# Eighteen of 22 pairs of ffn-up chunks as seven half-size products in place of eight

## The chip, the cores and the metric

The kernel runs on one core of a Trainium2 chip. The metric is the time of one execution on the device in microseconds (us); lower is better. Matrix products run on TensorE (PE in the profile; its weight loads are PEld), elementwise work on VectorE (DVE), ScalarE (ACT) and GpSimd (POOL). SP, the sync engine, issues most of the DMA transfers. Each engine takes its instructions in a fixed order and waits on semaphores for the others.

## The reference

The program is one step of a two-layer transformer for 128 context tokens and 512 latent tokens (640 columns in all, 1024 features). Each layer is an attention sub-layer and then a gated feed-forward layer ("ffn") with a width-3 convolution over the tokens:

```
def conv_ffn(u, w_up, conv_w, conv_b, w_down):
    z = u @ w_up                                   # 1024 -> 2 * 2816
    zp = jnp.pad(z, ((0, 0), (1, 1), (0, 0)))
    z = zp[:, :-2] * conv_w[0] + zp[:, 1:-1] * conv_w[1] + zp[:, 2:] * conv_w[2] + conv_b
    gate, val = jnp.split(z, 2, axis=-1)
    return (jax.nn.silu(gate) * val) @ w_down      # 2816 -> 1024
```

Its input u is the normalised residual stream h, scaled and shifted by vectors that depend on the conditioning ("adaLN"); its output is normalised, gated and added to h. The change touches z = u @ w_up alone.

## The kernel before

Activations lie with the features on the 128 partitions and the 640 tokens along the free axis, in eight chunks k of 128 features. All numbers are float32; a product keeps that precision by splitting each operand into a high part (a copy rounded to float32r, made by ACT) and a low part (operand minus high part, a subtraction of two SBUF operands on DVE or POOL): `split`, lines 160 to 162. Each product is then three matmuls, high by high, high by low, low by high.

The 2816 hidden features are 22 chunks of 128, each with a gate and a value chunk: a pair. `ffn_up` computes one pair. For each of its two chunks `chunks` loads 128x1024 weights, splits them (`load_w`), and `proj` runs 8 k times 3 matmuls times 2 halves of 320 tokens, 48 matmuls a chunk and 96 a pair, into one PSUM tile (`pu`). The input of these products is not yet normalised (class `Raw`), so `take` multiplies the result by the norm's reciprocal on DVE while it leaves PSUM, and ACT adds the shift. `conv` is one ACT instruction (line 1348) and six scalar_tensor_tensor on DVE (line 1356), which read `za` twice. After the second chunk: silu (ACT), gate times value (DVE, line 1387), and a split of the product g.

`ffn_down` follows part by part: the 22 pairs are cut into PARTS, the down product of a part (8 output chunks `dn`, n pairs times 6 matmuls each) stands behind the first pair of the next part, and its result is added to `yf` on DVE. The last part goes through `product` (`dl`) together with the closing norm and residual. `Pace` spreads the adaLN products (`ada`, weights `wm`) over the pairs.

A scheduler that has its own estimate of every instruction sets the order on each engine and the places in memory; the code's order is a priority to it. PSUM and SBUF tiles come from rings of a fixed count (`bufs`): raw weights `wr` 2 or 3, split weights `wh` and `wl` 3 each, adaLN weights `wm` 4.

Of the kernel before, what the change touches and what calls it, by code (L numbers as in the profile page):

```python
# [10 lines left out]
F32 = mybir.dt.float32  # L11
# [8 lines left out]
NCTX = 128  # L20
# [9 lines left out]
PARTS = [5, 6, 6, 5]  # L30
# [26 lines left out]
def tile_step(ctx: ExitStack, tc: tile.TileContext, a: dict):  # L57
# [9 lines left out]
    def dr(name, dt=F32):  # L67
        return dw(name, dt)[:, 0:1280]
# [77 lines left out]
    def load_w(src, n, name, kept=False, low=None):  # L146
        raw = wt("wr", f"wr_{name}")
        SP.dma_start(raw[:, :n], src)
        if kept:
            if n == 640:  # L150
                hl = dr(f"wk_{name}", F32R)
                hi, lo = hl[:, 0:n], hl[:, n : 2 * n]
            else:
                hi, lo = (dr(f"wk{v}_{name}", F32R) for v in range(2))
        else:
            hi, lo = wt("wh", f"wh_{name}", F32R), wt("wl", f"wl_{name}", F32R)
        split(raw[:, :n], hi[:, :n], lo[:, :n], low or DVE)
        return hi, lo
# [396 lines left out]
    def score_steps(pr):  # L555
# [17 lines left out]
        def dense(m, g):  # L573
# [6 lines left out]
            pd = wt(("wh", "wl")[g], f"p{pr.name}{m}{g}") if g < 2 else pr.kt4[:, m * 512 : m * 512 + 512]  # L580
# [791 lines left out]
    def ffn_up(l, u, c, first, pace):  # L1372
# [16 lines left out]
        split(t[0], g[:, 0:640], g[:, 640:1280])  # L1389
        return (g[:, 0:640], g[:, 640:1280])  # L1390
# [105 lines left out]
    for l in range(2):  # L1496
# [235 lines left out]
```

## Time and profile before

| | |
|---|---|
| runs | 1892.93, 1895.81, 1897.44 us, median 1895.81 us |
| the profiled execution | 1893.93 us, of which the span (first to last instruction) is 1891.8 us |
| busy: PE, PEld, DVE, ACT, POOL | 96%, 83%, 54%, 43%, 13% of the span |
| the ffn of layer 0 | about 504 to 945 us of the span |
| the ffn of layer 1 | about 1412 to 1838 us |

Busy time is the union of an engine's records. Matmuls are pipelined, so the mean duration of one (311 ns for 320 columns) is about twice the step from one to the next; the pace is read from a stretch, time by count. On DVE too an instruction's record begins a little before the one ahead of it ends when neither waits. PEclk is the TensorE clock that was granted, as a share of 2.4 GHz.

### The profile page before, as it was taken

The numbers are of one execution on the slowest core, as the hardware profiler recorded it, in microseconds if no ns is written. First come the engines' busy times: TensorE is split into PE (matmuls) and PEld (weight loads), VectorE is DVE, ScalarE is ACT, GpSimd is POOL, SyncE is SP. The second block draws the span as 40 slices with busy tenths as digits, with TensorE's granted clock in tenths as the row PEclk, the third lists the DMA queues.
The fourth block names the chain that finished last, engine by engine and source line by source line (L and its number), as shares of the span: only waits on it lengthen the run. The fifth ranks groups of instructions, "written<-read, shape, count | busy, mean of one in ns | idle before, by whom it ended". The sixth has DMA issues, their size and how long they took to land.

```text
span 1891.8 us, 28912 instructions
## 1 busy us (share of the span) xinstructions
PE 1818.3 (96%) x11619; PEld 1577.3 (83%) x11619; DVE 1025.9 (54%) x1776; ACT 806.2 (43%) x1325; POOL 253.9 (13%) x247
## 2 busy tenths in 40 slices
PE   7989799999999999999989998999999999999997
PEld 4888555569799999999978985456979999999996
DVE  3453454564663563663665644435467456466365
ACT  3433233255553451542465533324555345244245
POOL 0011243343100000000030003630220000000002
PEclk8999899999999999999999998999989999999999
DMA  7656564233133333333233364573412222222213
GB/s 254 195 159 219 146 184 119 77 128 140 68 96 96 114 104 121 124 120 101 95 104 126 116 212 147 167 205 113 152 67 86 94 79 65 82 78 62 84 58 105
DMA packets 84101, 229.88 MB, mean 122 GB/s; under 512 B 12224, under 2 KB 24896, under 8 KB 83968
## 3 DMA queue, kind: packets, MB, share of 16 engines
q1 hardware_dynamic: 74656, 209.73, 34.7%
q10 hardware_dynamic: 6720, 7.82, 1.5%
q0 software_dynamic: 2592, 10.49, 1.5%
q8 instruction: 91, 1.49, 0.3%
q14 instruction: 42, 0.34, 0.1%
HBM read 198.82 MB, written 28.06 MB: 120 GB/s over the span
## 4 chain that ended last, share of the span: by engine, by line
PE 81%; DVE 4%; issue 2%; DMA 2%; ACT 2%; POOL 1%; ACTq 0%; SPq 0%; POOLq 0%; DVEq 0%
PE pu L187 32%; PE dn L187 13%; PE op L187 2%; PE ada L321 2%; PE poD L638 2%; PE pnq L187 2%; PE pnk L187 1%; PE poG L638 1%; PE stM L569 1%; PE stG L569 1%; PE pqc L187 1%; PE poM L638 1%; PE stD L569 1%; PE dl L187 1%; PE op L166 1%
## 5 line engine op out<-in xcount | busy, mean ns | idle before, releaser
L187 PE MATMUL pu<-uop,wh_u 128*128 128x322 f32 (+1 forms) x2688 | 512.6, 312 | 0.0
L187 PEld LDWEIGHTS pu<-uop,wh_u 128*128 128x128 f32 x2688 | 428.7, 190 | 5.8 <-ACT wh_u L161 4.1
L187 PE MATMUL pu<-uop,wl_u 128*128 128x322 f32 x1344 | 308.2, 311 | 0.0
L1356 DVE SCALAR_TENSOR_TENSOR za<-za,cst 128x127 f32<-128x127 f32 (+1 forms) x528 | 193.1, 435 | 91.2 <-ACT za L1348 91.1
L187 PEld LDWEIGHTS pu<-uop,wl_u 128*128 128x128 f32 x1344 | 224.8, 188 | 0.0
L187 PE MATMUL dn<-g,wh_d 128*128 128x320 f32 x1088 | 203.8, 309 | 0.3 <-DVE cst L330 0.3
L291 POOL TENSOR_TENSOR cst<-cst 128x352 f32<-128x352 f32 (+4 forms) x42 | 48.1, 1145 | 1044.3 <-ACT cst L1427 1041.8
L187 PEld LDWEIGHTS dn<-g,wh_d 128*128 128x128 f32 x1088 | 170.8, 188 | 0.8 <-ACT wh_d L161 0.4
L161 ACT ACTIVATE wh_u<-wr_u 128x1024 fp32r<-128x1024 f32 x88 | 93.4, 1062 | 145.8 <-PE pu L187 73.0
L187 PE MATMUL dn<-g,wl_d 128*128 128x320 f32 x544 | 124.1, 309 | 0.0
L162 DVE TENSOR_TENSOR wl_u<-wr_u,wh_u 128x1024 fp32r<-128x1024 f32 x84 | 102.4, 1220 | 20.7 <-ACT wh_u L161 20.5
L437 ACT ACTIVATE za<-za,cst 128x128 f32<-128x128 f32 (+1 forms) x176 | 89.4, 556 | 22.8 <-DVE za L435 22.0
L187 PEld LDWEIGHTS dn<-g,wl_d 128*128 128x128 f32 x544 | 90.9, 188 | 0.0
L161 ACT ACTIVATE wh_d<-wr_d 128x768 fp32r<-128x768 f32 (+1 forms) x48 | 38.9, 811 | 113.1 <-PE dn L187 98.6
L1348 ACT ACTIVATE za<-za,cst 128x640 f32<-128x640 f32 x88 | 81.2, 923 | 3.0
L161 ACT ACTIVATE g<-za 128x640 fp32r<-128x640 f32 x44 | 32.5, 738 | 115.0 <-DVE za L1387 115.0
L434 DVE COPY cst<-pu 128x2 f32<-128x2 f32 x88 | 13.8, 157 | 124.0 <-PE pu L187 117.1
L1403 DVE TENSOR_TENSOR yf<-yf,dn 128x640 f32<-128x640 f32 x32 | 26.3, 821 | 94.7 <-PE dn L187 94.5
L1382 ACT ACTIVATE za<-za 128x640 f32<-128x640 f32 x44 | 32.5, 739 | 94.2 <-DVE za L1356 94.2
L435 DVE TENSOR_TENSOR za<-pu,rnuop 128x640 f32<-128x640 f32 x88 | 71.7, 815 | 0.0
L321 PE MATMUL ada<-wm,cst 128*32 128x256 f32 x768 | 63.1, 403 | 4.4 <-DMA wm<-in_wmod 2.4
L162 DVE TENSOR_TENSOR wl_op<-wr_op,wh_op 128x1024 fp32r<-128x1024 f32 x26 | 32.7, 1261 | 49.6 <-ACT wh_op L161 49.6
(581 smaller groups left out, 3478.8 us busy)
## 6 DMA issues: line engine op xcount, KB each, us to landing
wm<-in_wmod SPq DMA_DIRECT2D x96, 512.0 KB
wr_u<-in_w_up SPq DMA_DIRECT2D x88, 512.0 KB
wr_op<-in_w_o SPq DMA_DIRECT2D x26, 512.0 KB
wr_d<-in_w_dn SPq DMA_DIRECT2D x32, 384.0 KB
wr_dl<-in_w_dn SPq DMA_DIRECT2D x24, 320.0 KB
wr_d<-in_w_dn SPq DMA_DIRECT2D x16, 320.0 KB
h<-in_xT SPq DMA_DIRECT2D x4, 640.0 KB
hb<-in_xT SPq DMA_DIRECT2D x4, 640.0 KB
```

What stands on the lines that cost most here:

```text
L161: ACT.activation(hi, src, AF.Copy)
L162: low.tensor_tensor(lo, src, hi, op=ALU.subtract)
L187: PE.matmul(o[hf], w, xhalf(x, hf, e), start=start, stop=stop)
L291: POOL.tensor_tensor(sq_acc[:, cols], sq_acc[:, cols], sq[:, cols], op=ALU.add)
L321: PE.matmul(st["pt"][32 * j : 32 * j + 32, 0:256], silu_c[:, 4 * r + j, :], st[r][:, j * 256 : (j + 1) * 256], start=(r == 0), stop=(r == 1))
L435: DVE.tensor_tensor(dst, pview(pt, cut=cut), self.r, op=ALU.mult)
L437: ACT.activation(dst[:, s:e], dst[:, s:e], AF.Identity, bias=zb[:, ty : ty + 1])
L569: PE.matmul(out, kap[:, keys], qap[:, q], start=(i == 0), stop=(last and i == n - 1))
L638: PE.matmul(out[:, s:e], mp.v(kt), pj, start=(i == 0), stop=(i == 4))
L1348: ACT.activation(acc, z, AF.Identity, scale=cw[:, 1:2], bias=cw[:, 3:4])
L1356: DVE.scalar_tensor_tensor(acc[:, d0 : d0 + n], z[:, s0 : s0 + n], w, acc[:, d0 : d0 + n], op0=ALU.mult, op1=ALU.add)
L1382: ACT.activation(t[0], t[0], AF.Silu)
```

## The change

Pairs 0 to 3 stay as they are. From pair 4 on, the gate and value weights of a pair are seen as a 2x2 block matrix (gate or value by first or last four k) and the input as 2x2 blocks (first or last four k by first or last 320 tokens). Seven block products of sums and differences replace the eight block products (Strassen's scheme in Winograd's form). A block product is 4 k times 3 matmuls of 128x128 weights by 320 tokens, 12 matmuls, so a pair has 84 matmuls in place of 96.

- `operands` loads the two raw weight tiles and makes the seven left operands: three blocks as they are (a11, a12, a22, split by ACT and DVE) and four sums S1 to S4 (one POOL subtraction or addition each, split by ACT and POOL). So a pair issues 8 POOL instructions of 128x512 with two SBUF inputs, 7 ACT copies of 128x512 and 3 DVE subtractions of 128x512. They run two products ahead in the code's order (AHEADW).
- `ffn_up_seven` runs the seven products into PSUM tiles `x`, and puts them together with one ACT copy and seven DVE additions of 128x320 with one PSUM input. `take` is gone for these pairs. The convolution, the silu and the split of g are as before.
- `Blocks.prepare` makes the seven right operands once per layer, normalised and shifted, one k after each of pairs 0 to 3: 4 DVE scalar_tensor_tensor, 4 ACT shifts, 4 POOL subtractions of 128x320, and three splits (320 and 640 columns with the low part on DVE, 1280 with it on POOL).
- The residual h is written to HBM at the start of the ffn and read back as `hc` before the last down product.
- Parts become 5, 4, 4, 4, 5 pairs; the rings become `wr` 4, `wm` 2, `wh` 6 shared.

The core of the diff:

```diff
-PARTS = [5, 6, 6, 5]
+PARTS = [5, 4, 4, 4, 5]
+PLAIN = 4
+AHEADW = 2
...
-        return rp.tile([128, 1024], dt, tag=tag, name=name, bufs={"wr": 2, "wm": WMB}.get(tag, 3))
+        return rp.tile([128, 1024], dt, tag=tag, name=name, bufs={"wr": 4, "wm": 2, "wh": 6}[tag])
...
+        def prepare(self, k, h, r, A, Bv):
+
+            v = []
+            for c in (k, k + 4):
+                x, t = d2(h[c // 2])[:, c % 2, :], sq_tile(f"v{self.l}{c}").rearrange("p a b -> p (a b)")
+                for s, e, ty in ((0, NCTX, 0), (NCTX, NT, 1)):
+                    DVE.scalar_tensor_tensor(t[:, s:e], x[:, s:e], A[:, c, ty : ty + 1], r[:, s:e], op0=ALU.mult, op1=ALU.mult)
+                    ACT.activation(t[:, s:e], t[:, s:e], AF.Identity, bias=Bv[:, c, ty : ty + 1])
+                v.append(t)
+            f = dr(f"cf{self.l}{k}")
+            (b11, b12), (b21, b22) = ((t[:, 0:HALF], t[:, HALF:NT]) for t in v)
+            t1, t2, t3, t4 = (f[:, HALF * i : HALF * i + HALF] for i in range(4))
+            for out, x, y in ((t1, b12, b11), (t3, b22, b12), (t2, b22, t1), (t4, b21, t2)):
+                POOL.tensor_tensor(out, x, y, op=ALU.subtract)
...
+            split(b11, one[:, 0:HALF], one[:, HALF:NT])
+            split(v[1], two[:, 0:NT], two[:, NT : 2 * NT])
+            split(f, hi, lo, POOL)
...
+    def operands(l, c):
+
+        g, v = (wt("wr", f"wq{l}{c}{i}") for i in range(2))
+        SP.dma_start(g, a["w_up"][l, c])
+        SP.dma_start(v, a["w_up"][l, NFF + c])
+        a11, a12, a21, a22 = g[:, 0:512], g[:, 512:1024], v[:, 0:512], v[:, 512:1024]
...
+        def parts(n, x, low=DVE):
+            t = wt("wh", f"wx{n}{l}{c}", F32R)
+            split(x, t[:, 0:512], t[:, 512:1024], low)
+            return [(t[:, 128 * k : 128 * k + 128], t[:, 512 + 128 * k : 640 + 128 * k]) for k in range(4)]
+
+        yield parts("a11", a11)
+        s1, s2 = temp(1), temp(2)
+        POOL.tensor_tensor(s1, a21, a22, op=ALU.add)
+        POOL.tensor_tensor(s2, s1, a11, op=ALU.subtract)
+        yield parts("s2", s2, POOL)
+        POOL.tensor_tensor(a21, a11, a21, op=ALU.subtract)
+        yield parts("s3", a21, POOL)
+        yield parts("s1", s1, POOL)
+        yield parts("a12", a12)
+        yield parts("a22", a22)
+        POOL.tensor_tensor(s2, a12, s2, op=ALU.subtract)
+        yield parts("s4", s2, POOL)
+
+    def ffn_up_seven(l, u, c, stream, pace):
...
+        def prod(b):
+            ws = next(stream)
+            out = pq.tile([128, 512], F32, tag="x", name=f"x{b}{l}{c}", bufs=5)[:, 0:HALF]
+            for k in range(4):
+                mm3(out, ws[k], u.b[b][k], k == 0, k == 3)
+            return out
...
+        ACT.activation(g1, prod("11"), AF.Copy)
+        add(v, prod("t2"), g1)
+        add(w, prod("t3"), v)
+        x = prod("t1")
+        add(v2, x, w)
+        add(g2, x, v)
+        add(g1, prod("21"), g1)
+        add(v1, prod("t4"), w)
+        pace()
+        conv(zv, l, NFF + c, tv)
+        add(g2, prod("22"), g2)
+        conv(zg, l, c, tg)
+        ACT.activation(tg, tg, AF.Silu)
+        pace()
+        DVE.tensor_tensor(tg, tg, tv, op=ALU.mult)
...
+        h = [dr(f"hc{l}{i}") for i in range(4)]
+        for i in range(4):
+            SP.dma_start(d2(h[i]), hsrc[:, 2 * i : 2 * i + 2, :])
```

How the order stands. First VectorE in the middle of layer 0's ffn, before: from the product of pair 7 to the convolution of pair 8's gate (`za080` is the gate tile of layer 0, pair 8; `wl` are low parts of later weights).

```order
L1387 TENSOR_TENSOR za070_5161<-za070_5161,za071_5233 128x640
L162 TENSOR_TENSOR g07_5255<-za070_5161,g07_5255 128x640
L434 COPY cst_69<-pu080_5264 128x2
L435 TENSOR_TENSOR za080_5313<-pu080_5264,rnuop0_3625 128x640
L330 TENSOR_TENSOR cst_69<-ada023_5245,cst_69 128x4
L162 TENSOR_TENSOR wl_u091_5541<-wr_u091_5538,wh_u091_5540 128x1024
L349 TENSOR_TENSOR cst_69<-cst_69 128x8 x2
L1356 SCALAR_TENSOR_TENSOR za080_5313<-za080_5313,cst_69 128x127
L1356 SCALAR_TENSOR_TENSOR za080_5313<-za080_5313,cst_69 128x504
```

VectorE now, from the end of pair 6 to the convolution of pair 7's value (`za071`; `xt207` is the product with T2 of layer 0, pair 7, `wxa1108` the low part of pair 8's a11).

```order
L165 TENSOR_TENSOR wxa1108_5345<-wq080_5341,wxa1108_5345 128x512
L1490 TENSOR_TENSOR za060_5087<-za060_5087,za061_5088 128x640
L165 TENSOR_TENSOR g06_5248<-za060_5087,g06_5248 128x640
L1474 TENSOR_TENSOR za070_5251<-xt207_5274,za070_5251 128x320
L1474 TENSOR_TENSOR za070_5251<-xt307_5291,za070_5251 128x320
L1474 TENSOR_TENSOR za071_5252<-xt107_5308,za070_5251 128x320
L1474 TENSOR_TENSOR za070_5251<-xt107_5308,za070_5251 128x320
L1474 TENSOR_TENSOR za070_5251<-x2107_5327,za070_5251 128x320
L1474 TENSOR_TENSOR za071_5252<-xt407_5348,za070_5251 128x320
L165 TENSOR_TENSOR wxa1208_5452<-wq080_5341,wxa1208_5452 128x512
L1359 SCALAR_TENSOR_TENSOR za071_5252<-za071_5252,cst_69 128x127
L1359 SCALAR_TENSOR_TENSOR za071_5252<-za071_5252,cst_69 128x504
```

Two reads of PSUM per pair have become seven, and all of a pair's first six additions stand behind the whole tail (convolutions, product, g) of the pair before. Now GpSimd. Before, it has no instruction between the last low part of pair 0's weights and the first square of the last down product but three tiny ones:

```order
L162 TENSOR_TENSOR wl_u000_3608<-wr_u000_3605,wh_u000_3607 128x1024
L291 TENSOR_TENSOR cst_69<-cst_69 128x288
L162 TENSOR_TENSOR wl_u001_3614<-wr_u001_3611,wh_u001_3613 128x1024
L272 TENSOR_TENSOR cst_69<-cst_69 128x3 x3
L291 TENSOR_TENSOR cst_69<-cst_69 128x640
```

GpSimd now, in the same stretch of pairs 7 to 9 (`ws108` is the sum S1 of layer 0, pair 8, `wxs208` the low part of S2, `wq091` the raw value weights of pair 9).

```order
L1449 TENSOR_TENSOR ws208_5374<-ws108_5373,wq080_5341 128x512
L165 TENSOR_TENSOR wxs407_5324<-ws207_5215,wxs407_5324 128x512
L1448 TENSOR_TENSOR ws109_5537<-wq091_5506 128x512
L165 TENSOR_TENSOR wxs208_5377<-ws208_5374,wxs208_5377 128x512
L1451 TENSOR_TENSOR wq091_5506<-wq090_5505,wq091_5506 128x512
L1456 TENSOR_TENSOR ws208_5374<-wq080_5341,ws208_5374 128x512
L165 TENSOR_TENSOR wxs308_5418<-wq081_5342,wxs308_5418 128x512
L165 TENSOR_TENSOR wxs108_5435<-ws108_5373,wxs108_5435 128x512
L1449 TENSOR_TENSOR ws209_5538<-ws109_5537,wq090_5505 128x512
```

Eight such instructions a pair, all with two inputs from SBUF, and four of the seven weight operands end in one of them. Last, SP's queue before the last down product of layer 0 (`wr_dl06` is the weight tile of output chunk 6), before and now:

```order
L148 DMA wr_dl05_8284<-in_w_dn 128x640
L148 DMA wr_dl06_8311<-in_w_dn 128x640
L148 DMA wr_dl07_8337<-in_w_dn 128x640
L148 DMA wr_dl02_8364<-in_w_dn 128x640
L148 DMA wr_dl03_8390<-in_w_dn 128x640
```

And now (`hc` is the residual, read back):

```order
L151 DMA wr_dl06_8694<-in_w_dn 128x640
L1678 DMA hc00_8493<-hsf0_3786 128x1280
L1678 DMA hc01_8494<-hsf0_3786 128x1280
L1678 DMA hc02_8495<-hsf0_3786 128x1280
L1678 DMA hc03_8496<-hsf0_3786 128x1280
L151 DMA wr_dl07_8720<-in_w_dn 128x640
```

The four reads of h now stand between the loads `wr_dl06` and `wr_dl07`.

## Rows read from the trace of the kernel before

**Rows 1.** The page: busy shares, and the chain that ended last by engine.
```profile
PE 1818.3 (96%) x11619; PEld 1577.3 (83%) x11619; DVE 1025.9 (54%) x1776; ACT 806.2 (43%) x1325; POOL 253.9 (13%) x247
PE 81%; DVE 4%; issue 2%; DMA 2%; ACT 2%; POOL 1%; ACTq 0%; SPq 0%; POOLq 0%; DVEq 0%
```
**Rows 2.** The chain in order of time, layer 1's ffn: start, us, what.
```profile
1653.17 85.67 PE pu L187 x576
1738.84 42.29 PE dn L187 x288
```
**Rows 3.** Stretches: length, busy (count) of PE, PEld, DVE, ACT, POOL, clock, DMA.
```profile
1653.00:1739.00 86.00, 86.00 (x581) 86.00 (x580) 55.84 (x113) 42.15 (x57) 0.00 (x0) 1.00 0.21 68
1739.00:1781.00 42.00, 42.00 (x288) 42.00 (x288) 17.79 (x25) 9.59 (x13) 0.00 (x0) 1.00 0.28 88
```
**Rows 4.** Instructions by line and form: busy us, mean ns, idle before.
```profile
L1356 DVE SCALAR_TENSOR_TENSOR za<-za,cst 128x504 f32<-128x504 f32 x176 | 129.7, 737 | 0.0
L1356 DVE SCALAR_TENSOR_TENSOR za<-za,cst 128x127 f32<-128x127 f32 x176 | 61.2, 348 | 91.2 <-ACT za L1348 91.1
L162 DVE TENSOR_TENSOR ml<-pq,mh 128x512 fp32r<-128x512 f32 x4 | 2.7, 687 | 2.5 <-ACT mh L161 2.5
L1424 DVE TENSOR_TENSOR yf<-yf,dl 128x352 f32<-128x352 f32 x6 | 3.1, 519 | 3.4 <-PE dl L168 3.4
L1387 DVE TENSOR_TENSOR za<-za,za 128x640 f32<-128x640 f32 x44 | 36.3, 825 | 1.4
L1348 ACT ACTIVATE za<-za,cst 128x640 f32<-128x640 f32 x88 | 81.2, 923 | 3.0
L162 POOL TENSOR_TENSOR wl_u<-wr_u,wh_u 128x1024 fp32r<-128x1024 f32 x4 | 9.7, 2430 | 0.3 <-ACT wh_u L161 0.2
L321 PE MATMUL ada<-wm,cst 128*32 128x256 f32 x768 | 63.1, 403 | 4.4 <-DMA wm<-in_wmod 2.4 <-ACT psD L581 1.1 <-ACT psG L581 0.7
```
**Rows 5.** VectorE in order of time, one pair: start, us, what, idle before.
```profile
758.06 1.22 DVE L162 TENSOR_TENSOR wl_u<-wr_u,wh_u 128x1024 fp32r<-128x1024 f32 x1
760.19 2.19 DVE L1356 SCALAR_TENSOR_TENSOR za<-za,cst 128x127 f32<-128x127 f32 x6 [0.91 <-ACT za L1348]
...
771.19 0.82 DVE L162 TENSOR_TENSOR g<-za,g 128x640 fp32r<-128x640 f32 x1 [0.80 <-ACT g L161]
```
**Rows 6.** GpSimd in order of time, four places.
```profile
260.34 2.62 POOL L588 TENSOR_TENSOR acD<-acD,pD 128x512 f32<-128x512 f32 x2 [1.09 <-ACT pD L581]
...
440.42 1.44 POOL L291 TENSOR_TENSOR cst<-cst 128x352 f32<-128x352 f32 x1 [2.05 <-ACT cst L1427]
...
970.16 0.81 POOL L291 TENSOR_TENSOR cst<-cst 128x352 f32<-128x352 f32 x1 [1.54 <-ACT cst L1427]
...
986.70 3.06 POOL L162 TENSOR_TENSOR wl_oi<-wr_oi,wh_oi 128x1024 fp32r<-128x1024 f32 x1 [1.00 <-PE dl L168]
```
**Rows 7.** VectorE in order of time, at the last three of these places.
```profile
439.96 1.23 DVE L162 TENSOR_TENSOR wl_op<-wr_op,wh_op 128x1024 fp32r<-128x1024 f32 x1 [2.77 <-ACT wh_op L161]
...
969.76 0.52 DVE L1424 TENSOR_TENSOR yf<-yf,dl 128x352 f32<-128x352 f32 x1 [0.20 <-PE dl L168]
...
986.62 0.89 DVE L378 TENSOR_TENSOR hb<-hb,yf 128x704 f32<-128x704 f32 x1
...
987.80 2.11 DVE L426 SCALAR_TENSOR_TENSOR udl<-hb,cst,udl 128x128 fp32r<-128x128 f32 x1
```
**Rows 8.** Stretches around a gap on TensorE, layer 1's attention end.
```profile
1378.00:1382.00 4.00, 1.02 (x4) 0.22 (x2) 3.86 (x6) 1.06 (x3) 1.03 (x1) 0.99 0.50 187
1382.00:1386.00 4.00, 3.83 (x19) 2.10 (x22) 0.44 (x3) 1.58 (x5) 0.00 (x0) 0.50 0.00 1
```
**Rows 9.** SP's issues around layer 0's attention end and last down product.
```profile
418.70 4.55 SPq L1526 DMA_DIRECT2D hb<-in_xT  x4
...
939.32 33.34 SPq L148 DMA_DIRECT2D wr_dl<-in_w_dn  x9
```
**Rows 10.** The stretch of these four loads of 640 KB; last column GB/s.
```profile
412.00:425.00 13.00, 13.00 (x84) 12.01 (x81) 9.10 (x11) 5.00 (x9) 0.00 (x0) 1.00 0.72 246
```

More of the change, by code (lines that the diff above doesn't have):

```diff
@@ L155, in load_w @@
         else:
-            hi, lo = wt("wh", f"wh_{name}", F32R), wt("wl", f"wl_{name}", F32R)
+            hi, lo = (wt("wh", f"wh{v}_{name}", F32R) for v in range(2))
         split(raw[:, :n], hi[:, :n], lo[:, :n], low or DVE)
@@ L1389, in ffn_up, with __init__ @@
         split(t[0], g[:, 0:640], g[:, 640:1280])
+        return (g[:, 0:640], g[:, 640:1280])
+    class Blocks:
+        def __init__(self, l):
+            self.l, self.b = l, {n: {} for n in BLOCKS}
+        def prepare(self, k, h, r, A, Bv):
[11 more added lines that the diff above has]
+                POOL.tensor_tensor(out, x, y, op=ALU.subtract)
+            if k % 2 == 0:
+                self.one = dr(f"ub{self.l}{k}", F32R)
+            one = d2(self.one)[:, k % 2, :]
+            two = dr(f"ud{self.l}{k}", F32R)
+            hi, lo = (dr(f"ut{v}{self.l}{k}", F32R) for v in range(2))
+            split(b11, one[:, 0:HALF], one[:, HALF:NT])
+            split(v[1], two[:, 0:NT], two[:, NT : 2 * NT])
+            split(f, hi, lo, POOL)
+            self.b["11"][k] = (one[:, 0:HALF], one[:, HALF:NT])
+            for i, n in enumerate(("21", "22")):
+                self.b[n][k] = (two[:, HALF * i : HALF * i + HALF], two[:, NT + HALF * i : NT + HALF * i + HALF])
+            for i in range(4):
+                c = slice(HALF * i, HALF * i + HALF)
+                self.b[f"t{i + 1}"][k] = (hi[:, c], lo[:, c])
@@ new lines, in ffn_up_seven, with add @@
+    def ffn_up_seven(l, u, c, stream, pace):
+        zg, zv = (dw(f"za{l}{c}{i}") for i in range(2))
+        tg, tv = (z[:, NT : 2 * NT] for z in (zg, zv))
+        v, w = tg[:, 0:HALF], tg[:, HALF:NT]
+        g1, g2, v1, v2 = zg[:, 0:HALF], zg[:, HALF:NT], zv[:, 0:HALF], zv[:, HALF:NT]
+        def prod(b):
[4 more added lines that the diff above has]
+            return out
+        def add(out, x, y):
+            DVE.tensor_tensor(out, x, y, op=ALU.add)
+        ACT.activation(g1, prod("11"), AF.Copy)
[13 more added lines that the diff above has]
+        DVE.tensor_tensor(tg, tg, tv, op=ALU.mult)
+        g = dr(f"g{l}{c}", F32R)
+        split(tg, g[:, 0:640], g[:, 640:1280])
@@ L1532, in tile_step @@
         )
+        hsrc = scratch(f"hsf{l}", [128, 8, 640])
+        for i in range(4):
+            SP.dma_start(hsrc[:, 2 * i : 2 * i + 2, :], d2(h[i]))
         y = [dr(f"yf{l}{i}") for i in range(4)]
@@ L1536, in tile_step, with stream @@
         c, pend = 0, None
+        ub = Blocks(l)
+        def stream():
+            items = (x for c in range(PLAIN, NFF) for x in operands(l, c))
+            held = []
+            for x in items:
+                held.append(x)
+                if len(held) > AHEADW:
+                    yield held.pop(0)
+            yield from held
+        seven = stream()
         fill = adaln(l, 5) + [lambda: mod_gate(l, 1)]
@@ L1543, in tile_step @@
             for i in range(n):
-                gs.append(ffn_up(l, u, c, first if c == 0 else None, pace))
+                if c < PLAIN:
+                    gs.append(ffn_up(l, u, c, first if c == 0 else None, pace))
+                    for k in range(4):
+                        if k * PLAIN // 4 == c:
+                            ub.prepare(k, h, u.r, mA[l][1], modv[l][:, 24:32, :])
+                else:
+                    gs.append(ffn_up_seven(l, ub, c, seven, pace))
                 c += 1
@@ L1551, in tile_step @@
             f()
+        h = [dr(f"hc{l}{i}") for i in range(4)]
+        for i in range(4):
+            SP.dma_start(d2(h[i]), hsrc[:, 2 * i : 2 * i + 2, :])
         gs = pend[1]
```

11 lines of the change are left out of this document (7 added, 4 removed).

## The prediction

> **What bounds the kernel now.** I read the page's busy shares first, then the chain that ended last. TensorE is busy 96% of the span and holds 81% of the chain [rows 1]; VectorE has 54%, GpSimd 13%. In the feed-forward part the chain is matmuls without a break: 576 up-matmuls, six pairs, take 85.67 us, then 288 down-matmuls 42.29 us [rows 2]. So a step is 85.67 / 576 = 0.149 us, not the 0.31 us that a record lasts, and a pair of 96 matmuls costs 14.28 us. Over these six pairs VectorE is busy 55.84 of 86 us, 9.3 us a pair, and GpSimd not at all [rows 3]. The reader is to see that the change takes matmuls from the engine that is full, and gives work to two that have room by their busy shares. Whether they have it together is the question.
>
> **What goes from TensorE.** 36 pairs (18 a layer) lose 12 matmuls each: 432 x 0.149 = 64.3 us. A pair becomes 84 x 0.149 = 12.5 us. The down products keep their count (17 pairs in parts and 5 at the end, as before). If nothing else became late, the profiled execution would fall from 1893.9 to about 1830 us.
>
> **What a pair costs the other engines, each alone.** VectorE: the six convolution instructions of a chunk span 2.19 us [rows 5], although their records add up to more (737 and 348 ns [rows 4]); next to one another they step about 0.08 us less than they last, and I take that off each duration. Two convolutions: 4.38 us. Three low parts of 512 columns at 0.687 - 0.08: 1.83. Product and low part of g, 640 columns, at 0.825 - 0.08: 1.49. Seven additions of 320 columns with one input in PSUM: 352 columns took 0.519 [rows 4], so about 0.40 each: 2.8. Together 10.5 us. To this come waits for ScalarE inside a pair. Before each convolution VectorE waited 0.91 us and before the low part of g 0.80 [rows 5]; without the shift instructions only the 0.92 us of line 1348 [rows 4] is left before a convolution, less the 0.61 us low part that now stands there: 2 x 0.4 + 0.8 = 1.6 us. So 12.1 us, just under TensorE's 12.5. GpSimd: two additions of 512 columns back to back took 2.62 us [rows 6], so eight take 10.5 us. Each alone would fit.
>
> **They do not run beside each other.** This is the term that decides. GpSimd's addition of 352 columns took 0.81 us beside a VectorE addition with one input in PSUM; beside a subtraction with two SBUF inputs (439.96 to 441.19 us) the same form, started at 440.42, took 1.44: it finished 0.67 us after VectorE was done [rows 6, 7]. It works the other way too: VectorE's 128-column scalar_tensor_tensor of two SBUF operands at 987.80 lasted 2.11 us, until 0.15 us after GpSimd's low part ended (986.70 + 3.06 = 989.76), though a form of 127 columns has 0.35 us elsewhere [rows 4, 6, 7]. So instructions with two SBUF inputs on the two engines take turns; what is saved at a turn is the fixed part at the start, about 0.14 us on GpSimd's side and 0.2 on VectorE's. In before they hardly met. Now eight GpSimd instructions a pair (10.5 us) and 17 VectorE instructions (4.38 + 1.83 + 1.49 = 7.7 us) need turns: 18.2 us, less eight turns each way at 0.34: 15.5 us. That is the least a pair can take in a steady run of pairs. What queues behind: a VectorE low part or convolution that waits for its turn holds up the additions behind it, these hold the PSUM tiles `x`, and TensorE's next product waits for a tile; a GpSimd instruction that waits holds up the low parts of the next left operands, which TensorE waits for too. VectorE's additions from PSUM and its waits, 4.4 us, need no turn; if GpSimd has nothing ready just then, they come on top: 19.9 us. I take 17.0: GpSimd waits in its order for ScalarE's high parts and for free weight tiles, but four of seven operands run ahead, so a third of the 4.4 us.
>
> The Trainium skill, page "SBUF — State Buffer", section "Who interferes with whom", says that a VectorE instruction with two SBUF inputs contends with a GpSimd instruction that reads SBUF, and of contention that who is second blocks fully until the first has finished. The rows agree that the second waits, but show its start-up hidden. By the rule alone a pair would take the whole 18.2 us; that is the third rival below.
>
> **The sum for the feed-forward part.** A down product gives the pair behind it time: 192 or 240 matmuls at 42.29 / 288 = 0.147 us, 28 to 35 us in which VectorE has little else (17.79 of 42 us busy [rows 3]) and the first two products of that pair are made ready. I cost a group of four pairs between two down products as one pair at TensorE's pace with a microsecond of waiting, 13.5, and three at 17.0: 64.5 us, against 4 x 14.28 = 57.1. Four such groups a layer: +29.6 us (at 15.5: +11.6; at 19.9: +64).
>
> The first six pairs: pairs 0 to 3 get `prepare`. VectorE: four scalar_tensor_tensor (two of 128, two of 512 columns, 0.27 and 0.67 us) 1.9, low parts of 320 and 640 columns 1.15: 3 us. GpSimd: four of 320 columns at 0.81 x 320 / 352 = 0.74 [rows 6] and one of 1280 at 2.43 x 1.25 = 3.0 [rows 4]: 6 us. VectorE then has 9.3 + 3 us and waits of 2.6, plus some 1.6 us for turns: 16.5 against 14.3. Four pairs make 9 us, of which about 4 are lost behind the tiles that are ready at the start; pairs 4 and 5 add 12.5 + 17 - 28.6 = 1, and the last block of `prepare` about 3. So +8 a layer (0 to +20).
>
> **The smaller edits.** The four reads of h: four of 640 KB moved at 246 GB/s [rows 9, 10] take about 10.6 us, and stand in SP's queue between weight loads of the last down product, nine of which went out over 33 us [rows 9]. Cover is what the raised count of raw tiles holds ahead; if it is gone, up to 10 us a layer. I take 3. Writing h at the start is not waited for. The ring `wm` at 2: TensorE waited 2.4 us in all for adaLN weights [rows 4]; 0 to +10, I take 1. One more part a layer adds eight additions to `yf` beside matmuls: nothing, hidden by VectorE's room there. The other ring counts give as many weight tiles as before: nothing; the cover is the load ahead, and were it lost, each operand would show its high part's wait.
>
> Total: 1893.9 + 2 x (29.6 + 8 + 3) + 1 = 1976 us; the profiled execution is within the runs shown (median 1895.8), so I forecast 1975. The likeliest case's own range is 1920 (a pair at 15.5) to 2010.
>
> **The rivals.**
> (1) TensorE stays the bound. For it: each engine alone fits, the scheduler puts operands two products ahead, and GpSimd might take its turns in VectorE's gaps. Against it: turns of 15.5 us in 12.5. Groups 4 x (51 - 57.1), first pairs -4, h +3: 1893.9 - 2 x 25 + 1 = 1845. Chance 0.13.
> (2) The turns are packed nearly without gaps and the down products take more of them than I gave: the group falls to about 57, as before; with the first pairs and h about 1905. Chance 0.17, over 1880 to 1920. The break-even, with first pairs and h, is a pair of about 13.6 us; below it the kernel is faster.
> (3) Turns last the whole instruction: 13.5 + 3 x 18.2 = 68.1 a group, +11 each, 1893.9 + 2 x (44 + 8 + 3) + 1 = 2005. Chance 0.15.
> (4) The clock follows. After 4 us in which TensorE was busy 1.02 us, the granted clock stood at 0.50, its lower level of 1.2 GHz, with TensorE busy again [rows 8]. If the 4.5 us that a 17 us pair leaves idle come in one piece, part of each pair runs at half clock; no row prices that here, so I take the upper end, 19.9 us: 1893.9 + 2 x (64 + 20 + 5) = 2072. For it: all additions of a pair stand behind the tail of the pair before. Against: PSUM tiles spread the waits. Chance 0.13.
>
> **How the numbers follow.** The forecast has 0.42. The range of 8 in 10 reaches into the first and the fourth rival: 1870 to 2060. Less than 0.2% (4 us) this measurement can't tell from no change. Faster: rival 1 and a quarter of rival 2, 0.17; same: 0.04; slower: the rest, 0.79.
>
> **What would show it.** In the changed profile: up-matmuls fall from 4224 to 3792; in seven-product stretches TensorE is busy under 80% and waits for VectorE (low parts) and GpSimd (low parts of S1 to S4), or for PSUM tiles that VectorE reads; GpSimd's 512-column form has a mean well over 1.31 us, or VectorE's 504-column convolution well over 0.74; pairs come every 16 to 19 us, while the down products keep 0.148 us a matmul. The forecast is wrong if the two engines keep their durations beside each other, or if TensorE is over 95% busy in those stretches; the sizes are wrong if pairs come at 14 us or at 20.

## The result and the profile after

The changed kernel takes 2025.21 us (median of 4 runs, 2023.68 to 2027.30) against 1894.65 before: ratio 1.0688, 95% interval 1.067 to 1.0707. It is slower by 130 us although TensorE has 432 matmuls less. The forecast was 1975, with a range of 1870 to 2060.

The page of the changed kernel, busy shares and the chain that ended last, which answer to [rows 1]:

```profile
PE 1824.3 (90%) x11187; PEld 1550.3 (77%) x11187; DVE 1287.5 (64%) x2000; ACT 840.1 (42%) x1469; POOL 728.8 (36%) x575
...
PE 50%; DVE 28%; ACT 6%; issue 6%; DMA 3%; POOL 1%; ACTq 1%; SPq 0%; DVEq 0%; POOLq 0%
```

VectorE's part of the chain went from 4 to 28%, TensorE's from 81 to 50: the end no longer waits for TensorE alone. TensorE's busy time even rose by 6 us, because a matmul at the lower clock lasts longer (22 of them took 6.19 us at a clock of 0.50, in the stretch from 580 to 590 us below).

Two stretches of layer 1, with the columns of [rows 3]: four pairs with seven products and TensorE's wait behind them, and then a down product.

```profile
1815.00:1878.00 63.00, 51.59 (x334) 50.28 (x332) 55.54 (x82) 26.17 (x44) 43.15 (x30) 0.95 0.18 60
1884.00:1908.00 24.00, 24.00 (x166) 24.00 (x165) 10.65 (x15) 5.69 (x9) 2.79 (x3) 1.00 0.29 88
```

In the pairs TensorE is busy 82% of the time, VectorE 88%, GpSimd 68%; the down product runs as before (24.00 / 166 = 0.145 us a matmul). In the six stretches between one down product and the next TensorE is busy 82 to 91%. The wait behind the pairs, and the clock in it:

```profile
1878.31 5.87 PE L190 MATMUL dn<-g,wh_d 128*128 128x320 f32 x28 [7.13 <-DVE za L1474]
```

```profile
1876.00:1881.00 5.00, 2.69 (x10) 2.72 (x11) 4.95 (x12) 1.73 (x2) 0.00 (x0) 0.50 0.27 66
```

VectorE and GpSimd by line and form, answering to [rows 4, 6]:

```profile
L1359 DVE SCALAR_TENSOR_TENSOR za<-za,cst 128x504 f32<-128x504 f32 x176 | 184.3, 1047 | 0.0
L1359 DVE SCALAR_TENSOR_TENSOR za<-za,cst 128x127 f32<-128x127 f32 x176 | 110.3, 627 | 18.7 <-ACT za L1351 18.1
L165 DVE TENSOR_TENSOR wxa<-wq,wxa 128x512 fp32r<-128x512 f32 x108 | 109.8, 1029 | 22.6 <-ACT wxa L164 22.2
L1474 DVE TENSOR_TENSOR za<-xt,za 128x320 f32<-128x320 f32 x180 | 82.5, 483 | 22.3 <-PE xt L171 19.2
...
L165 POOL TENSOR_TENSOR wxs<-ws,wxs 128x512 fp32r<-128x512 f32 x108 | 157.0, 1454 | 127.0 <-ACT wxs L164 127.0
L1449 POOL TENSOR_TENSOR ws<-ws,wq 128x512 f32<-128x512 f32 x36 | 56.0, 1557 | 1.2
```

The same convolution instruction that lasted 737 ns lasts 1047; the short one 627 in place of 348; a low part of 512 columns 1029 in place of 687. All these read two SBUF tiles. The additions, with one input in PSUM, last 483 ns, as in every experiment below (480 to 486). So the instructions that the prediction made take turns grew, and these did not. One such turn, on VectorE and on GpSimd, in order of time (start, us, what, idle before):

```profile
1749.74 1.68 DVE L165 TENSOR_TENSOR wxa<-wq,wxa 128x512 fp32r<-128x512 f32 x1
1751.34 0.48 DVE L1474 TENSOR_TENSOR za<-x,za 128x320 f32<-128x320 f32 x1
1751.74 5.96 DVE L1359 SCALAR_TENSOR_TENSOR za<-za,cst 128x127 f32<-128x127 f32 x12
```

```profile
1749.58 1.29 POOL L165 TENSOR_TENSOR wxs<-ws,wxs 128x512 fp32r<-128x512 f32 x1
1750.94 1.62 POOL L1449 TENSOR_TENSOR ws<-ws,wq 128x512 f32<-128x512 f32 x1
1753.37 1.41 POOL L165 TENSOR_TENSOR wxs<-ws,wxs 128x512 fp32r<-128x512 f32 x1 [0.81 <-ACT wxs L164]
1759.13 1.65 POOL L165 TENSOR_TENSOR wxs<-ws,wxs 128x512 fp32r<-128x512 f32 x1 [4.34 <-ACT wxs L164]
```

VectorE's low part began 0.16 us after GpSimd's and ended at 1751.42, 0.55 us after GpSimd's (1750.87): it waited, with its start-up done beside the other (alone it takes 0.69 [rows 4]). Then two convolutions took 5.96 us in place of 2 x 2.19 [rows 5]. GpSimd meanwhile had nothing for 4.34 us: its next low part waited for ScalarE's high part. So the turns are not packed.

Where the 130 us lie, from the matmul records of each execution in order of time. "Six pairs" runs from the first up-matmul of a layer to its first down-matmul, "rest" (16 pairs and the down products between them) from there to the start of the last down product, "between" from there to the up-matmuls of layer 1. In the kernel before the up-matmuls begin at 482.1 and 1387.1 us, earlier than the 504 and 1412 us given above for the two ffn. Kernels of the experiments stand here too:

```
                              ffn 0   six pairs        rest             between
                              starts  layer 0, 1       layer 0, 1
before                        482.1    97.0   99.4     365.9  351.6     442.1
changed                       500.2   119.6  122.0     386.6  375.9     461.0
before, conditioning ring 2   497.3    96.9   98.6     368.4  351.6     461.8
all plain                     502.7    97.2   99.0     364.7  351.5     460.6
all plain, blocks prepared    498.0   101.4  101.2     364.8  351.5     459.5
no GpSimd sums                496.3   110.6  108.0     332.8  320.4     469.2
GpSimd with one input         495.7   114.2  109.9     338.7  330.9     467.4
six plain pairs               498.2   102.4  103.8     383.0  374.1     463.3
one ring of six               487.4   119.2  120.5     385.8  375.6     444.7
latent accumulators in PSUM   495.6   122.9  118.7     370.1  354.9     461.3
 + ring of six, six plain     484.1   102.3  102.9     369.8  358.9     442.5
 + context accumulators       484.6   102.3  100.6     338.2  337.4     446.0
 the last with four plain     482.5   122.6  119.9     337.6  331.3     447.2
```

Changed minus before: six pairs 22.6 + 22.6, rest 20.7 + 24.3, ahead and between 18.1 + 18.9, the tail (from the last down product of layer 1 on) 2.9: together 130.1, the difference of the spans (2021.9 and 1891.8).

The first 20 us after the plain pairs of layer 0, in stretches of 10 us, and the instructions of TensorE and of ScalarE there:

```profile
570.00:580.00 10.00, 3.62 (x13) 3.22 (x13) 10.00 (x10) 5.87 (x11) 7.68 (x5) 0.55 0.00 0
580.00:590.00 10.00, 6.19 (x22) 5.79 (x23) 8.73 (x14) 5.55 (x10) 5.61 (x5) 0.50 0.28 104
```

```profile
575.19 1.01 PE L331 MATMUL ada<-cst 128*128 128x2 f32 x4 [9.22 <-ACT cst L328]
580.86 0.63 PE L169 MATMUL x<-ub,wxa 128*128 128x320 f32 x1 [2.04 <-ACT ub L164]
```

```profile
573.60 1.27 ACT L164 ACTIVATE ut<-cf 128x1280 fp32r<-128x1280 f32 x1 [3.09 <-POOL cf L1415]
574.77 0.37 ACT L328 ACTIVATE cst<-ada 128x256 f32<-128x256 f32 x1
```

This is the seam between the plain pairs and the pairs with seven products. GpSimd's block subtractions `cf` are late; ScalarE's high part `ut` waits for them; behind it in ScalarE's order stands a small copy for the conditioning, and TensorE waits 9.22 us in its own order for that. Then it waits for the last prepared block. The granted clock falls to 0.50, the lower of its two levels. At the same place in layer 1 TensorE waits too, but for VectorE: 5.06 and 5.66 us, until VectorE has taken a plain pair's sum out of PSUM (line 438). So the wait lies at the same seam in both layers, and the instruction that it ends with is not the same.

### The profile page after: what moved, and what is told of

Read it like the earlier page. It is cut to its first block, busy times and chain, and to the rows that moved or that the text cites. A ratio compares the mean times of both kernels' runs of the same rounds, so it can differ in the third digit from the quotient of the medians.

```text
span 2021.9 us, 29200 instructions
## 1 busy us (share of the span) xinstructions
PE 1824.3 (90%) x11187; PEld 1550.3 (77%) x11187; DVE 1287.5 (64%) x2000; ACT 840.1 (42%) x1469; POOL 728.8 (36%) x575
## 4 chain that ended last, share of the span: by engine, by line
PE 50%; DVE 28%; ACT 6%; issue 6%; DMA 3%; POOL 1%; ACTq 1%; SPq 0%; DVEq 0%; POOLq 0%
DVE za L1359 13%; PE dn L190 12%; DVE za L1474 3%; PE op L190 2%; DVE wxa L165 2%; PE poD L641 2%; PE ada L324 2%; ACT za L1351 1%; PE pnq L190 1%; PE poG L641 1%; DVE za L1490 1%; DVE g L165 1%; PE stM L572 1%; PE xt L170 1%; PE xt L171 1%
## 5 line engine op out<-in xcount | busy, mean ns | idle before, releaser
L1359 DVE SCALAR_TENSOR_TENSOR za<-za,cst 128x127 f32<-128x127 f32 (+1 forms) x528 | 318.1, 671 | 18.7 <-ACT za L1351 18.1
L190 PEld LDWEIGHTS dn<-g,wh_d 128*128 128x128 f32 x1632 | 249.8, 195 | 27.7 <-issue 17.2
L165 POOL TENSOR_TENSOR wxs<-ws,wxs 128x512 fp32r<-128x512 f32 x108 | 157.0, 1454 | 127.0 <-ACT wxs L164 127.0
L169 PE MATMUL xt<-ut,wxs 128*128 128x320 f32 x432 | 136.6, 318 | 9.9 <-DVE za L438 5.7
L171 PE MATMUL xt<-ut,wxs 128*128 128x320 f32 x432 | 136.5, 316 | 2.9 <-POOL wxs L165 2.9
L170 PE MATMUL xt<-ut,wxs 128*128 128x320 f32 x432 | 136.8, 317 | 1.0 <-POOL ut L165 1.0
L165 DVE TENSOR_TENSOR wxa<-wq,wxa 128x512 fp32r<-128x512 f32 x108 | 109.8, 1029 | 22.6 <-ACT wxa L164 22.2
L1474 DVE TENSOR_TENSOR za<-xt,za 128x320 f32<-128x320 f32 x180 | 82.5, 483 | 22.3 <-PE xt L171 19.2
L190 PE MATMUL pu<-uop,wh_u 128*128 128x322 f32 x576 | 88.7, 316 | 5.3 <-DVE za L438 5.3
L169 PEld LDWEIGHTS xt<-ut,wxs 128*128 128x128 f32 x432 | 83.8, 195 | 11.8 <-issue 7.9
L190 PEld LDWEIGHTS pu<-uop,wh_u 128*128 128x128 f32 x576 | 87.9, 194 | 6.0 <-issue 6.0
L171 PEld LDWEIGHTS xt<-ut,wxs 128*128 128x128 f32 x432 | 83.8, 194 | 4.2 <-POOL wxs L165 4.2
L170 PEld LDWEIGHTS xt<-ut,wxs 128*128 128x128 f32 x432 | 84.0, 195 | 1.5 <-POOL ut L165 1.4
L164 ACT ACTIVATE wxs<-ws 128x512 fp32r<-128x512 f32 x108 | 67.3, 623 | 39.6 <-PE x L171 16.6
```

The source lines that it names most:

```text
L164: ACT.activation(hi, src, AF.Copy)
L165: low.tensor_tensor(lo, src, hi, op=ALU.subtract)
L169: PE.matmul(out, wh, xh, start=start, stop=False)
L170: PE.matmul(out, wh, xl, start=False, stop=False)
L171: PE.matmul(out, wl, xh, start=False, stop=stop)
L190: PE.matmul(o[hf], w, xhalf(x, hf, e), start=start, stop=stop)
```

## The experiments

Theory: VectorE's and GpSimd's instructions with two SBUF inputs take turns, and that sets the pace of the seven-product pairs. Rivals: VectorE's own chain, or GpSimd's place in the chain, is enough; the clock; and, for what the loops don't explain, the rings, the read-back of h, the preparing.

**Rings alone, in the kernel before.**

```diff
-bufs={"wr": 2, "wm": WMB}.get(tag, 3)
+bufs={"wr": 4, "wm": 2, "wh": 6}[tag]
```

> The kernel before with only the rings of weight tiles changed as the change has them: four raw tiles, two for the conditioning (wm, from 4) and six shared for high and low parts, in place of 2, 4, 3 and 3. The prediction's step (conditioning ring +1, other rings nothing): 1896, at most 1905. Rival, that the 37 us which the changed kernel is longer outside the two feed-forward loops come from the rings: about 1930. With the span before feed-forward 0 of the first layer at 482 us by the step and at 500 us by the rival.

1926.51 us, ratio 1.0171 (1.0145 to 1.0196). The rival was right: +31, not +1.

**One ring alone.**

```diff
-WMB = 4
+WMB = 2
```

> The kernel before with one number changed: two buffers in place of four for the conditioning weights. The prediction's step for it was +1 (0 to 10): 1897. The rings together cost 31 us; if this ring is the cause, 1915-1930, the loss lying ahead of feed-forward 0 and in the second layer's attention. Rival, the raw-weight ring of four (earlier loads of other weights on the same queue) or the shared high and low parts: 1893-1900 here.

1932.40 us, ratio 1.0198 (1.016 to 1.0236). The conditioning ring by itself costs 37.6 us; the other ring counts cost nothing beside it. SP's queue waits at the loads of the conditioning weights, before and with two tiles (total us, times, longest):

```profile
SPq L315 <- PE ada L321: 122.6, 31, 16.0
...
SPq L315 <- DMA wm<-in_wmod: 4.0, 4, 2.2
```

```profile
SPq L315 <- PE ada L321: 186.4, 50, 16.0
SPq L315 <- DMA wm<-in_wmod: 39.3, 21, 3.4
```

And the stretch from 200 to 300 us, before and with two tiles:

```profile
200.00:300.00 100.00, 85.12 (x421) 49.23 (x420) 56.74 (x91) 34.55 (x59) 42.38 (x35) 0.93 0.61 175
```

```profile
200.00:300.00 100.00, 84.58 (x381) 50.35 (x379) 52.05 (x83) 30.70 (x51) 38.37 (x32) 0.85 0.61 168
```

TensorE's own waits for these weights grew only from 2.4 [rows 4] to 8.5 us. SP's queue, which issues most loads, waited 99 us more for this ring, and in the attention TensorE did 40 matmuls less in these 100 us, busy as long but at a lower clock. That the price is paid in small pieces by what stands behind in SP's order is a reading of these rows; no run took it apart.

**The ring mended, in the changed kernel.**

```diff
+tag = "wr" if tag == "wm" else tag
-bufs={"wr": 4, "wm": 2, "wh": 6}[tag]
+bufs={"wr": 6, "wh": 6}[tag]
```

> The changed kernel with one edit: raw weights and conditioning weights take their tiles from one ring of six, in place of four and two, so that an attention stage, which loads few raw weights at once, can have more than two conditioning tiles under way. If the conditioning ring is what the changed kernel loses outside its loops, 30 to 37 us come back: 1988-1997, with feed-forward 0 beginning near 482-486 us in place of 500. Rival, the loss comes from where the scheduler puts the conditioning work, not from buffers: 2015 or more.

1993.95 us, ratio 1.0508 (1.0474 to 1.0541): 31 us back with as many tiles as the change has, 29 of them at the two places where they were lost ("ffn 0 starts" and "between" in the table).

**All pairs plain.**

```diff
-PLAIN = 4
+PLAIN = 22
-if k * PLAIN // 4 == c:
+if False:
```

> The changed kernel with all 22 pairs plain and no prepared blocks: left of the change are the rings, the down products in five parts of 5, 4, 4, 4, 5, and the residual stream spilled and read back. The prediction's steps add up to +7 (rings +1, read-back +3 a layer): about 1902. Rival, that what lies outside the loops (37 us) comes with these: about 1932, and if the first kernel of this set is at 1896 it is the read-back or the parts, not the rings.

1927.79 us, ratio 1.0167 (1.0145 to 1.0188): the same as with the rings alone. The read-back of h and the fifth part cost nothing that can be measured.

**All pairs plain, blocks prepared** (`if k == c:` in place of `if False:`).

> As the kernel with all pairs plain, but the blocks and their sums are prepared beside the first four pairs of each layer as the change does it, and then not used. The prediction's step: 8 us a layer (0 to 20) over the kernel with all pairs plain, so about +16. Rival, that the first stretch's +23 a layer in the changed kernel is all preparing: +45. If it is less than +23 the rest of that stretch belongs to its first two pairs from seven products and to filling their operands' ring.

1940.71 us, ratio 1.0233 (1.02 to 1.0266): 13 us more than with all pairs plain by the runs, but the six pairs grew by only 4 and 2 us, and the two profiled spans are 1.5 us apart. Between 2 and 13, then, below the prediction's 16; that preparing alone costs 45 is excluded.

**GpSimd's sums left out.**

```diff
-s1, s2 = temp(1), temp(2)
-POOL.tensor_tensor(s1, a21, a22, op=ALU.add)
...
+for _ in range(3):
+    yield p11
```

> The changed kernel without the sums of the weight blocks: the four operands made on GpSimd are left out, with their sums, high and low parts, and the first operand's parts stand in for three of them and the last for the fourth; the products, PSUM sums and convolutions stay, the output is another. Turns between VectorE and GpSimd (the theory): with GpSimd idle in the loops a pair falls from 15.5 to 12.5-13 us, VectorE's convolution instruction of 504 columns back to about 0.74 us from 1.05, and the time by 2.5 to 3 us for each of 36 pairs, to 1920-1940. Rival, VectorE's own chain of sums and its waits for ScalarE set the pace whatever GpSimd does: a pair stays at 15 or more, time 2000 or more. Third: TensorE's clock falls with the gaps; then the granted clock in the loops rises with this kernel and the rest stays.

1892.67 us, ratio 0.9984 (0.997 to 0.9999): 132 us less than the changed kernel, more than expected. The rest of a feed-forward part lost 54 and 56 us, 3.4 a pair; the six pairs another 9 and 14. A stretch of pairs of layer 1, and the convolution:

```profile
1632.00:1682.00 50.00, 50.00 (x343) 50.00 (x342) 37.04 (x81) 17.93 (x28) 0.00 (x0) 1.00 0.23 74
```

```profile
L1359 DVE SCALAR_TENSOR_TENSOR za<-za,cst 128x504 f32<-128x504 f32 x176 | 133.9, 761 | 0.0
```

TensorE is full, the granted clock is 1.00, and the convolution is back at 761 ns. VectorE's own chain does not set the pace, and without gaps the clock does not fall.

**GpSimd kept as busy, with one input.**

```diff
-POOL.tensor_tensor(s1, a21, a22, op=ALU.add)
+POOL.tensor_scalar(s1, a21, 1.0, None, op0=ALU.mult)
...
-split(x, t[:, 0:512], t[:, 512:1024], low)
+ACT.activation(t[:, 0:512], x, AF.Copy)
+POOL.tensor_scalar(t[:, 512:1024], x, 1.0, None, op0=ALU.mult)
```

> The changed kernel with all eight GpSimd instructions of a pair kept in place, size and order, each reading one tile of SBUF (a scaled copy) in place of two, so that the four operands are not the sums they should be; ScalarE's high parts stay too. Turns between two-input instructions (the theory): VectorE's convolution of 504 columns stays near 0.74 us, a pair at 12.5-13.5, the time 1890-1925. Rival, GpSimd's place in the chain (each operand must come through it in turn, whatever it reads) sets the pace: the time 1980 or more, with PE waiting for GpSimd's tiles. If GpSimd's copies are themselves much shorter than 1.3 us the two are told apart only by VectorE's durations where they overlap.

1914.88 us, ratio 1.0101 (1.0069 to 1.0133). Four pairs of layer 1, the convolution and one of GpSimd's copies:

```profile
1644.00:1693.00 49.00, 49.00 (x337) 49.00 (x335) 39.69 (x76) 26.19 (x44) 46.49 (x30) 1.00 0.23 76
```

```profile
L1359 DVE SCALAR_TENSOR_TENSOR za<-za,cst 128x504 f32<-128x504 f32 x176 | 144.5, 821 | 0.0
...
L1445 POOL TENSOR_SCALAR wxs<-ws 128x512 fp32r<-128x512 f32 x108 | 173.6, 1612 | 23.3 <-PE xt L171 13.6 <-issue 3.5 <-PE x L171 2.5
```

This tells the theories apart. GpSimd's instructions are no shorter (1612 ns, against 1454 in the changed kernel), it is busy 95% of the stretch, and all four operands still come through it; yet TensorE is full. One more thing differs: the copy that stands for a low part does not read ScalarE's high part, so GpSimd's waits for ScalarE are gone as well (127.0 us before one group of low parts in the changed kernel, in the rows above). VectorE's own durations and the experiments with PSUM, where GpSimd waits for ScalarE as before, settle that it was the second input. Each VectorE instruction of 504 columns was held against GpSimd's records: in the changed kernel the 110 that no GpSimd instruction overlaps last 734 ns on average, the 64 that one overlaps by over 0.3 us 1595. With one-input copies 110 are overlapped so, and they last 873, half of them under 740. The rest, 821 against 761 ns over all, is what one-input copies still cost VectorE.

**VectorE's second input moved to PSUM.** The accumulators of the 512 latent columns, and the product of gate and value, go to two PSUM banks.

```diff
-conv(zv, l, NFF + c, tv)
+pg, pv = (pq.tile([128, 512], F32, tag="cv", name=f"cv{i}{l}{c}", bufs=CVB) for i in range(2))
+conv7(zv, l, NFF + c, tv, pv)
...
-DVE.tensor_tensor(tg, tg, tv, op=ALU.mult)
+DVE.tensor_tensor(pv, tg[:, L:NT], pv, op=ALU.mult)
```

> The changed kernel with the convolution's accumulators of the 512 latent columns, and the gate-value product, in PSUM, so that the long VectorE instructions of a pair read one SBUF tile and not two (the temporary ring of the sums is two in place of three to make room). Turns theory: of 10.5 us of VectorE a pair some 3.5 still take turns with GpSimd's 10.5, 14 in all, and the convolution of 504 columns falls from 1.05 to about 0.75 us; a pair at 13 to 14 us from 15.5, the time 1940-1975. Rival, VectorE's own chain: the split adds four short instructions a pair, so 2025 or more.

1979.33 us, ratio 1.0431 (1.0396 to 1.0467): 46 us back, a little less than expected.

```profile
L166 DVE TENSOR_TENSOR wxa<-wq,wxa 128x512 fp32r<-128x512 f32 x108 | 127.7, 1189 | 17.8 <-ACT wxa L165 17.1 <-issue 0.2
L1370 DVE SCALAR_TENSOR_TENSOR za<-za,cst 128x127 f32<-128x127 f32 x144 | 111.3, 774 | 19.6 <-ACT za L1367 17.4
L1372 DVE SCALAR_TENSOR_TENSOR cv<-za,cst,cv 128x504 f32<-128x504 f32 x144 | 103.6, 739 | 0.1
```

The long convolution is free of turns (739 ns, and 738 where GpSimd overlaps it by over 0.3 us), but the waiting moved to what still reads two SBUF tiles: low parts 1189 from 1029, the short convolution 774 from 627.

**Six plain pairs, in the changed kernel.**

```diff
-PLAIN = 4
+PLAIN = 6
```

> The changed kernel with one number changed: six plain pairs a layer in place of four, so that the four preparations lie beside pairs 0, 1, 3 and 4 and pair 5 lies between the last one and the first product that needs it. If the wait for the last prepared blocks at the first seven-product pair is what the first stretch loses, the six pairs of a layer fall from 120-122 us to about 102, and the time by 30 to 40 to 1985-1995, although four pairs fewer have seven products. Rival, the preparing itself fills VectorE and GpSimd and only the turns of two pairs a layer go: 5 less, 2018-2023.

1983.82 us, ratio 1.0449 (1.0408 to 1.0491): 41 us back, 17 and 18 of them in the six pairs. Where the seam was, plain pairs go on:

```profile
560.00:570.00 10.00, 9.82 (x66) 9.03 (x66) 6.99 (x14) 6.11 (x11) 2.74 (x4) 0.83 0.53 172
570.00:580.00 10.00, 10.00 (x70) 10.00 (x69) 9.17 (x21) 5.62 (x10) 0.68 (x1) 1.00 0.12 34
```

What covers the last preparation is not pair 5, as was expected, but the first down product, which with six plain pairs stands between the last of them and the first pair with seven products. TensorE, and then GpSimd with the last prepared block:

```profile
600.61 35.37 PE L190 MATMUL dn<-g,wh_d 128*128 128x320 f32 x240
635.81 0.31 PE L169 MATMUL x<-ub,wxa 128*128 128x320 f32 x1
```

```profile
601.40 2.96 POOL L165 TENSOR_TENSOR ut<-cf,ut 128x1280 fp32r<-128x1280 f32 x1 [1.39 <-ACT ut L164]
```

The block's low part is ready at 604.36 us, 3.75 us into the down product; without the 35 us of that product TensorE might have had to wait here again.

**The three mended together** (latent accumulators in PSUM, one ring of six, six plain pairs).

> As the kernel with accumulators in PSUM, and two more edits: raw weights and conditioning weights share one ring of six (as many tiles as the change's four and two), and six plain pairs a layer in place of four, so that the prepared blocks are ready before the first product needs them. From the runs: rings -31 if the shared ring gives the conditioning its room back, the wait at the first seven-product pair about -9 a layer, two plain pairs more +1 to +3 a layer by what a pair then gains: 1885-1935. Rival, the loss outside the loops comes from order, not from buffers: about 1950.

1915.84 us, ratio 1.01 (1.0072 to 1.0129). The ring came back as reckoned (30 us at its two places), the seam about twice as far (21 and 16 us in the six pairs, against 9 a layer). Pairs that follow one another without a down product still start 12.9 to 19.4 us apart, with VectorE over 90% busy:

```profile
1719.00:1772.00 53.00, 47.21 (x316) 45.93 (x315) 49.80 (x84) 27.89 (x53) 39.32 (x30) 1.00 0.19 59
```

**The context accumulators in PSUM too.**

```diff
-conv7(zv, l, NFF + c, tv, pv)
+pc = pq.tile([128, 512], F32, tag="cc", name=f"cc{l}{c}", bufs=CCB)
+conv7(zv, l, NFF + c, cv, pv)
```

with `cg`, `cv` two slices of `pc`, and the down products in tiles `x` to make room.

> As the kernel with six plain pairs, shared ring and latent accumulators in PSUM, with the accumulators of the 128 context columns in PSUM too, and the down products after the first part in the products' PSUM tiles to make room for that. Left with two SBUF inputs on VectorE are three low parts of weights a pair. Turns theory: the four short convolution instructions fall from 0.78 to about 0.37 us, VectorE gains 1.6 us a pair and is no longer over 90% busy, a pair comes to 12.5-13.2 from about 13.9: 16 pairs a layer, 1916 minus 20 to 40, so 1876-1896. Rival, fewer PSUM tiles for products make TensorE wait: 1916 or more.

1863.85 us, ratio 0.9838 (0.979 to 0.9885): faster than the kernel before by 1.6%, and better than expected.

```profile
1596.00:1645.00 49.00, 49.00 (x336) 49.00 (x335) 43.37 (x91) 30.34 (x58) 40.71 (x30) 1.00 0.21 65
```

```profile
L1373 DVE SCALAR_TENSOR_TENSOR cc<-za,cst,cc 128x127 f32<-128x127 f32 x128 | 44.9, 351 | 4.7 <-ACT cc L1370 3.8
L1375 DVE SCALAR_TENSOR_TENSOR cv<-za,cst,cv 128x504 f32<-128x504 f32 x128 | 94.5, 742 | 0.1
```

GpSimd does all its sums (40.71 of 49 us), with the same dependence on ScalarE as in the changed kernel, and a pair takes 49.00 / 4 = 12.25 us: TensorE's pace. What is left are some 4 us at each down product of layer 1: TensorE waits about 2 us there for its weights' parts, and the granted clock falls to 0.50 behind that. It was not followed up.

**The same with four plain pairs.**

> The same with four plain pairs a layer as in the change. Two more pairs a layer gain 1 to 1.8 us each (4 to 7 in all), the wait for the last prepared blocks comes back at the first pair (9 us a layer in the kernel without GpSimd's sums): 10 to 18 us slower than the kernel with six. Rival, the wait was of VectorE's and GpSimd's turns and has gone with them: 4 to 7 faster.

1898.65 us, ratio 1.0017 (0.9997 to 1.0037): 35 us slower, twice what was expected. It lies in the six pairs (20 and 19 us more, with 24 matmuls less). The seam stays when the convolutions of the pairs with seven products are out of the turns. The preparing and the convolutions of the plain pairs still read two SBUF tiles, so turns at the seam itself are not excluded.

## Why the prediction was right, and where its sizes were off

- **What bounds.** Right. 4224 up-matmuls became 3792, and their 64 us are real where TensorE is full: 49.00 us for 336 matmuls is 0.146 each. They were lost because it was not full.
- **Turns.** Right, and shown from both sides: with GpSimd idle, or busy with one input, a pair falls to TensorE's pace; with VectorE's second inputs in PSUM it falls too, step by step. GpSimd's means of 1.38 to 1.56 us and the convolution's 1.05 are two of the signs that the prediction asked for. Two others just failed: TensorE was busy 82 to 91% between down products, not under 80, and a pair took 15.7 us on average, not 16 to 19. The Trainium skill, page "SBUF — State Buffer", section "Who interferes with whom", has whole-instruction turns between a VectorE instruction with two SBUF inputs and any GpSimd instruction that reads SBUF. That the second waits is what the rows show; that its start-up also waits is not (0.55 us behind the other's end, where alone it takes 0.69), and for a GpSimd instruction with one input the run with copies shows hardly any turns.
- **A group of four pairs.** Predicted 64.5 against 57.1 us, +29.6 a layer; measured +20.7 and +24.3, so about 62.7 a group and 15.7 us a pair, the down product's help in it. Slightly too dear. The shape was another, too: behind each of the last three down products of layer 1's parts the pairs start 12.3, 12.3 and 18.7 us apart, and the next down product begins after a wait (of 7 us in the row shown). So two pairs, not one, run at TensorE's pace, and the waiting comes at the end of the group; why it does was not followed up.
- **The first six pairs.** Predicted +8 a layer (0 to 20), measured +22.6: the mis-sized term of the mechanism. VectorE's and GpSimd's work for the blocks was about right: 4 us were left of it in the prediction, and pairs that only carry it grow by 2 to 4. What failed is "the last block of `prepare` about 3": the prediction costed when the block is ready, not what stands in order behind it. Six plain pairs, with a down product behind the last block, take 17 to 18 us of it away. Leaving out GpSimd's sums takes 9 and 14 us away, of which two pairs with seven products at 3.4 each make 7, so turns may have a share in the seam; how large it is stays open.
- **The ring `wm`.** Predicted +1 (0 to 10), measured +31 to +38: the largest miss. The step was taken from TensorE's 2.4 us of waiting for these weights, but with two tiles SP's queue waits 99 us more, and what stands behind in its order waits with it.
- **Read-back of h, the fifth part.** Predicted +6 and 0; measured nothing.
- **The sum.** 59 + 16 + 1 + 6 = 82 predicted; 45 + 45 + 37, and 3 in the tail, make 130 measured. The likeliest case's own range ended at 2010; the time fell beyond it and into the wide one, for the ring and the seam and not for the reasons of the rivals. The wide range reached so far up for the sake of the clock, so that it held the time is in part luck; that the change is slower, and by which mechanism, is not.
- **Rivals.** TensorE stays the bound (1845): false here, true of the kernel with all accumulators in PSUM. Packed turns (1905, although the prediction's own terms add up to 1917): false, a group does not fall to 57, and GpSimd waits for ScalarE between its turns. Whole-instruction turns (2005): nearer in time by accident; a group is below even the 64.5. The clock (2072): a part of the price, not the whole. Its mean between down products is 0.93 to 0.97, and behind a wait it falls to 0.50 for some us, in the pairs as at the seam. An estimate from the matmul records and the granted clock (busy time by the share that is not granted): about 12 us in each layer's rest, beside 38 us in which TensorE stands idle. Without the gaps both go: 1.00 in the kernel without GpSimd's sums.

## What to carry to other kernels

Two engines with room by their busy shares may not have it together: before giving both more work, count the instructions on either that read two SBUF tiles, and move an accumulator to PSUM where that takes an input away. A ring is priced by the queue that waits for its tiles and by all that is queued behind, not by the waits of the engine that uses them. Where one stage prepares for the next, put a stretch of unrelated work (here a down product) between the last preparation and the first use, or the engines that take their work in order wait for one another at the seam.

## What the runs showed that was not expected

- GpSimd's one-input scaled copy of 512 columns (1.56 to 1.61 us) lasts longer than its two-input addition (2.62 / 2 = 1.31 [rows 6]), and yet it hardly disturbs VectorE.
- Taking the long instructions out of the turns lengthened the short ones that stayed (348 ns before, 627 changed, 774 with the long ones in PSUM, 351 when they were in PSUM themselves).
- Two buffers in place of four, in a ring for which TensorE waited 2.4 us in all, cost 2% of the time.
- TensorE did not slow down evenly: behind three down products of layer 1 two pairs ran at its full pace (12.3 us) before the turns showed in the next (18.7).
